# A bidirectional RWKV-7 layer on one Trainium2 core: copies ordered by PSUM bank, gate and residual rows fetched at the head of a round, and a fixed place for the loads of a stage

## The chip, the cores and the metric

The kernel runs on one core of one Trainium2 chip. The metric is the device time of one execution in microseconds (us), as the median of several runs. The engines are TensorE (PE, matmuls; PEld is its weight load), VectorE (DVE), ScalarE (ACT), GpSimd (POOL) and SyncE (SP), which here only issues DMAs. DMAs are also issued from the queues of ACT and POOL. An engine works through its own instructions in the order in which they stand; between engines there are only waits for data or for a buffer that has to come free.

## What is computed

One layer: an input projection, token shifts, a short convolution with gates, a two-way RWKV-7 scan over 128 context and 2048 latent tokens (8 heads of 64), and an output projection with a residual and a norm. The part that matters here is the scan:

```python
def step(S, inp):
    r_t, w_t, k_t, v_t, kk_t, a_t = inp
    s_kk = jnp.einsum('bdhij,bdhj->bdhi', S, kk_t)
    S = (S * w_t[..., None, :] - s_kk[..., :, None] * (kk_t * a_t)[..., None, :]
         + v_t[..., :, None] * k_t[..., None, :])
    return S, jnp.einsum('bdhij,bdhj->bdhi', S, r_t)
...
y = ys[:, 0] + jnp.flip(ys[:, 1], axis=1)
mean = jnp.mean(y, axis=-1, keepdims=True)
var = jnp.mean(jnp.square(y - mean), axis=-1, keepdims=True)
y = ((y - mean) * lax.rsqrt(var + GN_EPS)).reshape(b, t, A_WIDTH)
y = y * lp['gn_w'].astype(f32) + lp['gn_b'].astype(f32)
...
ya = ya.astype(x.dtype) * jax.nn.silu(g_a)
```

The kernel forms the scan by chunks of 64 tokens. Within a chunk the recurrence is a triangular system; its inverse is made once, and the state S then goes from chunk to chunk by matmuls.

## The kernel before

The program has three stages in time. The first makes the projections and spills the scan's operands to DRAM. The second is the scan. The third is the output projection; part of its matmuls (tile `psa`) is strewn into the scan to fill TensorE.

The scan is 17 stages (index s), each of 8 chunks in each of the two directions for one pair of heads (one of the 17 holds the context). A stage's parts are generators:

- `partL` (line 892) issues the loads of a stage's operands: `o` (two transfers of 512 KB, from `scr_ops`, line 907) and `a` (two of 128 KB, from `scr_lo`, line 914). They go into one of three sets of buffers, by s modulo 3.
- `partI` (917) loads the triangles (`ab`, four transfers, line 950) and solves them on GpSimd (`solve_steps`, 957; lines 960 to 980), which writes the inverse `scr_zt`. The buffer alternates between two, so the load for solve k waits until GpSimd is done with solve k-2. `partI(s + 7)` stands at the end of round s.
- `partW` (1036) makes two products: psF, masked by DVE into F (1066), and psG. A psG lies in two PSUM banks, one for each direction (`psG_0`, `psG_1`). DVE multiplies one half of each bank by a mask (1073, two instructions a bank), ACT copies the other half (1076, recorded at 846, two instructions a bank).
- `partU` (1079) transposes the inverse, multiplies it with `a` into psU; ACT copies psU into `zr` (1091, two instructions), and psW is the next product, from `zr`. psW is copied by ACT into `zb` (1101, recorded at 844).
- `partB` (1108) makes psX and four psE a half, masked by DVE (1136) and copied by ACT into `E`.
- `partS` (1140) is the chain over the chunks: psS from `sv` and `E`, then DVE scales psS into the next chunk's `sv` (1173).
- `finish` (1198) works up the output of one block: it fetches the gate rows `sg` (1215) and, three steps later, the residual rows `q` (1233, into a tile with the tag `w`), squares on ACT (1224), normalises on DVE (1227 to 1231), transposes on TensorE (psT), multiplies by the gate (1244, into a tile `yo`), adds q (1246) and stores to `scr_mixT` (1250).

A round s of the scan plays a list of letters (`ORDER`, 758): L is a step of partW(s+1), u and U of partU(s+1), b and B of partB of s and s+1, S of partS(s), `f`, `T` and `Y` steps of `finish`, a the projection's matmuls. Matmuls are kept in the order in which they were written (`pin`, `mm`), and some DMAs and ACT instructions are held behind the last matmul written (`now`). Such a tie is for the scheduler alone, which lays out each engine's order from a model of time; on the chip it is no wait. What isn't tied goes where the scheduler's model sees room.

In this text the rounds are numbered by s. In the trace, the psU of round 5 starts at 1140.3 us, of round 8 at 1216.1, of round 9 at 1240.6, of round 10 at 1270.8 and of round 11 at 1295.8.

Of the kernel before, what the change touches and what calls it, by code (L numbers as in the profile page):

```python
# [748 lines left out]

ROUND = "L b L u U S f b S b U S c b S c b L B L T S c B S B Y S c B S B".split()  # L750
ROUND_W = "L b L u U S f b S c b U S c b S c b c L B L T S B c S B Y c S B c S c B".split()
ROUND_M = "m L b L u U S f b S c b U S c b S b L B L T S B c S B Y c S m B S B".split()
ROUND_FILL = "L b a a L u U S f b S b U S b S b m L B a a L T S B S B Y S B S B".split()
ROUND_MORE = "m L b a a L u U S a a f b S b U S b S b L B a a L T S a a B S m Y B S B S B".split()
ROUND_ATT = "w m L b a a L u U S a a f b S b U w S b S b L B a a L T S a a B S m Y B S B S B".split()
ROUND_END = "w m L b a a L u U S a a f b S b U w S b b S L B a a L a a T w S B Y m S B S B w S B B".split()
ROUND_LAST = "f a a S w b S a x b S w a b T Y x S a b x".split()
ORDER = [ROUND, ROUND_W, ROUND_M] + [ROUND_FILL] * 10 + [ROUND_MORE, ROUND_ATT, ROUND_END, ROUND_LAST]
# [3 lines left out]
def phase2(K):  # L762
# [129 lines left out]
    def partL(s, after=None):  # L892
        st = Ctx()
        st.g = []
        st.low = B.low[s % LA]
        for gi, (d, units, blk) in enumerate(stages[s]):
            g = Ctx()
            st.g.append(g)
            g.d, g.units, g.blk = d, units, blk
            g.ops = B.ops[s % LA][d]  # L900
            src = S[f"ops{d}"][0:4:3]
            if blk is None:
                for k in range(2):
                    D(g.ops[:, k].rearrange("p (g u) t -> p g (u t)", u=2), src[k, :, 0:128].rearrange("(g p) t -> p g t", p=128))
            else:
                p, c0 = units[0]
                D(g.ops[:].rearrange("p k u t -> p k (u t)"), src[:, p * 128:(p + 1) * 128, c0 * 64:(c0 + 8) * 64].rearrange("k p t -> p k t"))
        for gi, g in enumerate(st.g):
            src = S["lo"][g.d]
            if g.blk is None:  # L910
                D(st.low[:, gi].rearrange("r (p u) i -> r p (u i)", u=2), src[:, 0:2].rearrange("(p r) u i -> r p (u i)", r=128))
            else:
                p, c0 = g.units[0]
                behind(D(st.low[:, gi], src[p * 128:p * 128 + 128, c0:c0 + 8]), after)
        return st
# [120 lines left out]
    def partW(s, st):  # L1036
# [7 lines left out]
        for n in range(2):  # L1044
# [22 lines left out]
            yield  # L1067
            ps = product(1, 0, "G")
            for gi, g in enumerate(st.g):
                us = half(g, n)  # L1070
                for h in range(2):
                    r = place(g.d, h)
                    V.tensor_tensor(g.gs[H[1 - h], g.op, h, us], ps[gi][r, :, 64:128], B.mG[r, g.d].unsqueeze(1).broadcast_to((64, 4, 64)), ALU.mult)  # L1073
                for h in range(2):
                    r = place(g.d, h)
                    copy(g.gs[H[1 - h], 0, h, us], ps[gi][r, :, 0:64])
            yield

    def partU(s, st):
# [10 lines left out]
        for r0, r1 in rows:  # L1090
            copy(zr[r1], pu[r1])
        yield
# [105 lines left out]
    def finish(p, blk, y):  # L1198
# [84 lines left out]
    def main():  # L1283
# [9 lines left out]
        for _ in range(3):  # L1293
            next(bb)
        sts[LA] = partL(LA, K.first)
        partI(7, O.solved)
        tail = iter(())
        side = dict(a=K.fill(), c=K.conv_weights(), m=K.mixes(), w=K.att_weights(), x=K.first_mixes())
        for s in range(NST):
# [8 lines left out]
            def play(tokens):  # L1308
                for c in tokens:
                    if c == "f":  # L1310
                        for f in todo:
                            for _ in range(3):
                                next(f, None)
                    elif c in "TY":
                        for f in todo:
                            next(f, None)
                    else:
                        next(gens[c])
                        if c == "S":
                            next(tail, None)  # L1320
# [3 lines left out]
            else:  # L1324
# [320 lines left out]
```

## Time and profile before

| | |
|---|---|
| runs | 1591.10, 1594.23, 1593.82 us (median 1593.82) |
| the profiled execution | 1593.89 us, its span 1592.1 us |
| TensorE busy | 1509.6 us (95%) |
| VectorE, ScalarE, GpSimd busy | 1120.7, 772.5, 586.8 us |
| granted TensorE clock | 0.984 of full speed, mean |
| DMA | 336.67 MB, 211 GB/s over the span |

The page and the views name an instruction by its line in the kernel, its engine and its tiles (out<-in). "x4" is a count; a time in brackets is how long the engine stood idle before it, and the arrow names what ended that. The SPq rows of the timeline are DMAs being issued, not the transfers themselves. `scr_...` are the scratch tensors in DRAM.

### The profile page before, as it was taken

What the parts mean: (1) busy time and instruction counts of PE and PEld (TensorE: products, weight loads), DVE (VectorE), ACT (ScalarE), POOL (GpSimd) and SP (SyncE); (2) the same over time, 40 slices, a digit from 0 to 9 for tenths busy, and PEclk for the clock granted to TensorE, in tenths of its full rate; (3) what the DMA queues carried; (4) which work ended last, traced back from release to release, by engine and by line L of the source; (5) the groups of instructions that cost most, each with busy time, mean ns of one, the idle gap of its engine ahead of it and who ended that gap; (6) DMA issues with size and microseconds to landing.
All of it is one profiled execution on the core that took longest, in us unless ns stands there. A gap on an engine that the chain in (4) does not pass through costs nothing.

```text
span 1592.1 us, 42472 instructions
## 1 busy us (share of the span) xinstructions
PE 1509.6 (95%) x17160; PEld 1382.9 (87%) x17160; DVE 1120.7 (70%) x2246; ACT 772.5 (49%) x1645; POOL 586.8 (37%) x1030
## 2 busy tenths in 40 slices
PE   6899999999999999999999989989999999999997
PEld 3799988999999999999989889977888788877886
DVE  5875978785646866757878788557677576677773
ACT  4553655462515453525535401566766666663331
POOL 0011212120202121202286567388888883012431
PEclk9899999999999999999999999999999999999999
DMA  9686758766555656464684976777676676558751
GB/s 376 199 297 219 266 188 303 254 224 234 166 171 171 205 177 217 164 214 171 208 256 158 282 233 208 211 205 213 182 209 191 192 203 188 138 160 314 247 177 66
DMA packets 242355, 336.67 MB, mean 211 GB/s; under 512 B 91688, under 2 KB 192296, under 8 KB 228080
## 3 DMA queue, kind: packets, MB, share of 16 engines
q1 hardware_dynamic: 233616, 323.27, 63.7%
q10 hardware_dynamic: 7344, 6.76, 1.4%
q0 software_dynamic: 1200, 3.93, 0.7%
q8 instruction: 135, 2.21, 0.6%
q14 instruction: 60, 0.49, 0.1%
HBM read 212.64 MB, written 121.26 MB: 210 GB/s over the span
## 4 chain that ended last, share of the span: by engine, by line
PE 44%; POOL 10%; DVE 8%; DMA 4%; ACT 3%; issue 3%; SPq 0%; DVEq 0%; ACTq 0%; POOLq 0%
PE psu L1446 7%; POOL zt L975 5%; POOL ztmp L972 3%; PE psE L855 3%; PE psS L855 2%; PE psa L1446 2%; PE mmg L166 1%; PE mmg L167 1%; PE mmg L168 1%; PE mmc L166 1%; PE mmc L167 1%; PE mmv L166 1%; PE mmv L167 1%; PE mmc L168 1%; PE mmv L168 1%
## 5 line engine op out<-in xcount | busy, mean ns | idle before, releaser
L975 POOL TENSOR_TENSOR zt<-zt,ztmp 128x30 f32<-128x30 f32 (+7 forms) x390 | 156.9, 402 | 30.6
L855 PE MATMUL psE<-fg 128*64 128x128 f32 x2176 | 147.6, 278 | 2.0 <-issue 2.0
L855 PEld LDWEIGHTS psE<-fg 128*64 128x64 f32 x2176 | 120.9, 140 | 6.0 <-issue 4.0
L855 PE MATMUL psS<-sv,E 128*64 128x64 f32 x2176 | 95.5, 229 | 21.7 <-DVE sv L1173 16.2
L329 POOL TENSOR_TENSOR shk<-rawl 128x384 f32<-128x384 f32 (+1 forms) x24 | 25.2, 1049 | 243.1 <-ACT rawl L325 223.2
L855 PEld LDWEIGHTS psS<-sv,E 128*64 128x64 f32 x2176 | 81.2, 140 | 35.0 <-DVE sv L1173 23.5
L846 ACT COPY E<-psE 128x256 f32<-128x256 f32 x136 | 50.0, 372 | 103.2 <-DVE E L1136 90.6
L1073 DVE TENSOR_TENSOR fg<-psG,consts 64x256 f32<-64x256 f32 x136 | 57.4, 422 | 55.7 <-PE psG L855 53.7
L972 POOL TENSOR_TENSOR ztmp<-ab,zt 128x60 f32<-128x60 f32 (+4 forms) x165 | 87.0, 527 | 12.9
L844 ACT ACTIVATE fg<-psX 64x512 f32<-64x512 f32 x136 | 80.5, 592 | 20.3 <-PE psX L855 17.8
L1446 PE MATMUL psu<-woh,mha 128*128 128x512 f32 x272 | 88.9, 396 | 0.0
L1570 POOL TENSOR_TENSOR z<-z,x 128x512 f32<-128x512 f32 x32 | 47.4, 1482 | 93.7 <-DVE z L1566 45.4
L329 POOL TENSOR_TENSOR shv<-rawl 128x384 f32<-128x384 f32 (+1 forms) x24 | 21.2, 882 | 162.5 <-ACT rawl L325 162.3
L1136 DVE TENSOR_TENSOR E<-psE,consts 128x256 f32<-128x256 f32 x136 | 56.6, 417 | 30.3 <-PE psE L855 28.6
L1173 DVE TENSOR_TENSOR sv<-psS,pc 64x128 f32<-64x128 f32 x262 | 65.8, 276 | 16.0 <-PE psS L855 14.1
L446 POOL COPY pcs<-pp 128x6 f32<-128x6 f32 (+1 forms) x48 | 25.0, 523 | 137.3 <-ACT pp L435 133.4
L846 ACT COPY fg<-psG 64x256 f32<-64x256 f32 x136 | 49.8, 366 | 49.0 <-DMA fg<-scr_ops 17.6
L166 PE MATMUL mmc<-h,w 128*128 128x384 f32 (+1 forms) x192 | 65.3, 340 | 5.9 <-ACT q1r L327 4.1
L166 PE MATMUL mmg<-h,w 128*128 128x384 f32 (+1 forms) x192 | 64.2, 334 | 3.8 <-ACT q1v L327 3.8
L167 PE MATMUL mmc<-h,w 128*128 128x384 f32 (+1 forms) x192 | 64.6, 336 | 0.0
L166 PE MATMUL mmb<-h,w 128*128 128x384 f32 (+1 forms) x192 | 62.9, 328 | 1.5 <-ACT ta L439 1.5
L166 PE MATMUL mmgb<-h,w 128*128 128x384 f32 (+1 forms) x192 | 64.0, 333 | 0.3 <-ACT q1r L327 0.3
(316 smaller groups left out, 5083.3 us busy)
## 6 DMA issues: line engine op xcount, KB each, us to landing
w<-scr_wsp SPq DMA_DIRECT2D x68, 1024.0 KB, 6.0
scr_wsp<-w SPq DMA_DIRECT2D x34, 1024.0 KB, 5.7
scr_ops<-pair SPq DMA_DIRECT2D x80, 384.0 KB, 3.9
wr<-in_win SPq DMA_DIRECT2D x34, 512.0 KB, 6.0
o<-scr_ops SPq DMA_DIRECT2D x32, 512.0 KB, 5.3
fg<-scr_ops SPq DMA_DIRECT2D x120, 128.0 KB, 3.8
x<-in_x SPq DMA_DIRECT2D x17, 512.0 KB, 3.5
wadas<-in_wada SPq DMA_DIRECT2D x8, 1024.0 KB, 9.9
```

What stands on the lines that cost most here:

```text
L166: T.matmul(ps[:, :n], w[:, 0, k], hh[:, 0, k, :n], start=k == 0, stop=False)
L167: T.matmul(ps[:, :n], w[:, 0, k], hh[:, 1, k, :n], start=False, stop=False)
L168: K.dense = T.matmul(ps[:, :n], w[:, 1, k], hh[:, 0, k, :n], start=False, stop=k == 7).ins
L844: P.activation(dst, src, AF.Copy, scale=-1.0)
L846: P.copy(dst, src)
L855: r = T.matmul(*a, start=True, stop=True, **k)
L972: eng.tensor_tensor(tv, ab[:, j:j + 2, j + 2:32].unsqueeze(1).broadcast_to((128, kn, 2, n)), zt[:, :kn, j:j + 2].unsqueeze(3).broadcast_to ...
L975: last = eng.tensor_tensor(zt[:, :kn, j + 2:32], zt[:, :kn, j + 2:32], tv[:, :, r], ALU.subtract).ins
L1073: V.tensor_tensor(g.gs[H[1 - h], g.op, h, us], ps[gi][r, :, 64:128], B.mG[r, g.d].unsqueeze(1).broadcast_to((64, 4, 64)), ALU.mult)
L1136: V.tensor_tensor(to(H[1]), of(H[1]), B.mE[:, g.d].unsqueeze(1).broadcast_to((128, 4, 64)), ALU.mult)
L1173: r = V.tensor_tensor(dst, sp[gi][0:64, q], B.pc[0:64, d, 2 * p:2 * p + 2, c:c + 1].broadcast_to((64, 2, 64)), ALU.mult)
L1446: r = T.matmul(ps[:], l[:, c], r, start=start and n == x == 0, stop=stop and n == 3 and x == 2)
```

## The change

Four edits.

1. **psG and psU on ACT.** The copies of a psG bank are tied behind that bank's masks, the next bank's masks behind the first's, and U's copies of psU behind the last of G's copies.
2. **finish.** `sg` and `q` are fetched together in a step of their own, which a new letter `g` at the head of a round plays. `q` gets a tile of its own (tag `yo`), and the product that went into `yo` goes back into the tile of `sg`, from which it is stored.
3. **The loads of a stage.** The call `partL(s + 4)` at the end of round s becomes `partL(s + 3)` at a new letter `P` in the middle of round s; the early call for stage 3 goes.
4. **Ties.** The loads of `o` and `a` are held behind the last matmul written, as other DMAs were.

```diff
-ROUND_FILL = "L b a a L u U S f b S b U S b S b m L B a a L T S B S B Y S B S B".split()
+ROUND_FILL = "g L b a a L u U S f b S b U S b S b m L B a a L T P S B S B Y S B S B".split()
...
-                D(g.ops[:].rearrange("p k u t -> p k (u t)"), src[:, p * 128:(p + 1) * 128, c0 * 64:(c0 + 8) * 64].rearrange("k p t -> p k t"))
+                now(D(g.ops[:].rearrange("p k u t -> p k (u t)"), src[:, p * 128:(p + 1) * 128, c0 * 64:(c0 + 8) * 64].rearrange("k p t -> p k t")))
...
-                behind(D(st.low[:, gi], src[p * 128:p * 128 + 128, c0:c0 + 8]), after)
+                r = D(st.low[:, gi], src[p * 128:p * 128 + 128, c0:c0 + 8])
+                behind(r, after)
+                now(r)
...
+            st.masked = None
             for gi, g in enumerate(st.g):
                 us = half(g, n)
                 for h in range(2):
                     r = place(g.d, h)
-                    V.tensor_tensor(g.gs[H[1 - h], g.op, h, us], ps[gi][r, :, 64:128], B.mG[r, g.d].unsqueeze(1).broadcast_to((64, 4, 64)), ALU.mult)
+                    m = V.tensor_tensor(g.gs[H[1 - h], g.op, h, us], ps[gi][r, :, 64:128], B.mG[r, g.d].unsqueeze(1).broadcast_to((64, 4, 64)), ALU.mult)
+                    behind(m, st.masked)
+                    st.masked = m.ins
                 for h in range(2):
                     r = place(g.d, h)
-                    copy(g.gs[H[1 - h], 0, h, us], ps[gi][r, :, 0:64])
+                    st.copied = P.copy(g.gs[H[1 - h], 0, h, us], ps[gi][r, :, 0:64])
+                    behind(st.copied, st.masked)
...
-            copy(zr[r1], pu[r1])
+            behind(P.copy(zr[r1], pu[r1]), st.copied.ins if O.line else None)
...
-        sg = place("sg")
+        sg, q = place("sg"), place("yo")
...
         fetch("sg", sg)
+        fetch("q", q)
+        yield
...
-        q = place("w")
-        fetch("q", q)
...
-        o = place("yo")
+        o = sg
...
-        sts[LA] = partL(LA, K.first)
...
+                    if c == "P":
+                        if s + LA < NST:
+                            sts[s + LA] = partL(s + LA)
+                    elif c == "g":
+                        for f in todo:
+                            next(f)
...
-            if s + LA + 1 < NST:
-                sts[s + LA + 1] = partL(s + LA + 1)
```

TensorE's and GpSimd's instructions stand in the same order as before, and DVE's too but for a few neighbours in the last rounds. What moves is on ACT and on SP.

ACT, around the psU of round 8 (`fg` is where psG's copies go, `zr` where U's go, `w` and `yss` belong to finish), before:

```order
L1224 ACTIVATE w_15278<-y_13845 128x512
L846 COPY fg_9817<-psG_0_0_15201 64x256 x2
L846 COPY zr_15227<-psU_15229 32x512 x2
L846 COPY fg_9818<-psG_1_0_15202 64x256 x2
L1228 ACTIVATE yss_15280<-yss_15280,geps 128x8
```

and of the change:

```order
L1232 ACTIVATE w_15271<-y_13839 128x512
L1081 COPY fg_9817<-psG_0_0_15196 64x256 x2
L1081 COPY fg_9818<-psG_1_0_15197 64x256 x2
L1097 COPY zr_15222<-psU_15224 32x512 x2
L1236 ACTIVATE yss_15273<-yss_15273,geps 128x8
```

The two copies of psG's second bank now stand ahead of U's two copies; so it is in 15 of the scan's rounds.

SP, from the end of round 8 into round 9 (`ab` are the triangles for a solve on GpSimd, `sg` and `w<-scr_q` the gate and residual rows for finish, `a` and `o` a stage's operands), before:

```order
L907 DMA o_9813<-scr_ops_58 128x2x512
L1250 DMA scr_mixT<-yo_15495 128x512
L1023 DMA fg_9817<-scr_ops_57 64x2x256
L1012 DMA sv_15658<-scr_vt 64x1024
L950 DMA ab_1099_15593<-scr_at 32x1x1024 x4
L1012 DMA sv_15660<-scr_vt 64x1024
L1023 DMA fg_9817<-scr_ops_57 64x2x256
L1023 DMA fg_9818<-scr_ops_58 64x2x256 x2
L914 DMA a_10979<-scr_lo 128x256
L1213 DMA sg_15791<-scr_sg 128x512
L914 DMA a_10979<-scr_lo 128x256
L1213 DMA w_15800<-scr_q 128x512
```

and of the change:

```order
L907 DMA o_9816<-scr_ops_58 128x2x512
L914 DMA a_10980<-scr_lo 128x256 x2
L1256 DMA scr_mixT<-sg_15130 128x512
L1025 DMA fg_9817<-scr_ops_57 64x2x256
L1219 DMA sg_15644<-scr_sg 128x512
L952 DMA ab_1093_15583<-scr_at 32x1x1024 x4
L1219 DMA yo_15645<-scr_q 128x512
L1014 DMA sv_15652<-scr_vt 64x1024
L1014 DMA sv_15654<-scr_vt 64x1024
L1025 DMA fg_9817<-scr_ops_57 64x2x256
L1025 DMA fg_9818<-scr_ops_58 64x2x256 x2
```

`sg` now stands ahead of `ab` and `q` right behind it; both were at the end of this piece. `a` has gone up to `o`. In two of the rounds (4 and 8) `sg` stands behind `ab` too.

SP, at the start of the scan (`a` and `o` of stages 1 to 4, `ab` of solve 6), before:

```order
L907 DMA o_10977<-scr_ops_57 128x2x512
L907 DMA o_10978<-scr_ops_58 128x2x512
L587 DMA scr_mixT<-ob_5_10789 128x320
L914 DMA a_10979<-scr_lo 128x256 x2
L914 DMA a_10980<-scr_lo 128x256 x2
L950 DMA ab_11007<-scr_at 32x1024 x4
L914 DMA a_9814<-scr_lo 128x256 x2
```

and of the change:

```order
L907 DMA o_10977<-scr_ops_57 128x2x512
L907 DMA o_10978<-scr_ops_58 128x2x512
L587 DMA scr_mixT<-ob_5_10789 128x320
L914 DMA a_10979<-scr_lo 128x256 x2
L907 DMA o_9815<-scr_ops_57 128x2x512
L907 DMA o_9816<-scr_ops_58 128x2x512
L914 DMA a_10980<-scr_lo 128x256 x2
L952 DMA ab_11007<-scr_at 32x1024 x4
```

The two `o` of stage 2 come here between the `a` of stages 1 and 2; before, they and those of stage 3 were issued some 15 to 50 us earlier, beside the end of the projections. The two of stage 3 now come later in round 0.

More of the change, by code (lines that the diff above doesn't have):

```diff
@@ L747 @@
 LA = 3
-ROUND = "L b L u U S f b S b U S c b S c b L B L T S c B S B Y S c B S B".split()
-ROUND_W = "L b L u U S f b S c b U S c b S c b c L B L T S B c S B Y c S B c S c B".split()
-ROUND_M = "m L b L u U S f b S c b U S c b S b L B L T S B c S B Y c S m B S B".split()
-ROUND_FILL = "L b a a L u U S f b S b U S b S b m L B a a L T S B S B Y S B S B".split()
[L754 to L757, printed above, removed]
+ROUND = "g L b L u U S f b S b U S c b S c b L B L T P S c B S B Y S c B S B".split()
+ROUND_W = "g L b L u U S f b S c b U S c b S c b c L B L T P S B c S B Y c S B c S c B".split()
+ROUND_M = "g m L b L u U S f b S c b U S c b S b L B L T P S B c S B Y c S m B S B".split()
+ROUND_FILL = "g L b a a L u U S f b S b U S b S b m L B a a L T P S B S B Y S B S B".split()
+ROUND_MORE = "g m L b a a L u U S a a f b S b U S b S b L B a a L T P S a a B S m Y B S B S B".split()
+ROUND_ATT = "g w m L b a a L u U S a a f b S b U w S b S b L B a a L T S a a B S m Y B S B S B".split()
+ROUND_END = "g w m L b a a L u U S a a f b S b U w S b b S L B a a L a a T w S B Y m S B S B w S B B".split()
+ROUND_LAST = "g f a a S w b S a x b S w a b T Y x S a b x".split()
 ORDER = [ROUND, ROUND_W, ROUND_M] + [ROUND_FILL] * 10 + [ROUND_MORE, ROUND_ATT, ROUND_END, ROUND_LAST]
@@ L903, in partL @@
                 for k in range(2):
-                    D(g.ops[:, k].rearrange("p (g u) t -> p g (u t)", u=2), src[k, :, 0:128].rearrange("(g p) t -> p g t", p=128))
+                    now(D(g.ops[:, k].rearrange("p (g u) t -> p g (u t)", u=2), src[k, :, 0:128].rearrange("(g p) t -> p g t", p=128)))
             else:
                 p, c0 = units[0]
-                D(g.ops[:].rearrange("p k u t -> p k (u t)"), src[:, p * 128:(p + 1) * 128, c0 * 64:(c0 + 8) * 64].rearrange("k p t -> p k t"))
+                now(D(g.ops[:].rearrange("p k u t -> p k (u t)"), src[:, p * 128:(p + 1) * 128, c0 * 64:(c0 + 8) * 64].rearrange("k p t -> p k t")))
         for gi, g in enumerate(st.g):
@@ L1309, in play @@
                 for c in tokens:
-                    if c == "f":
+                    if c == "P":
[4 more added lines that the diff above has]
+                            next(f)
+                    elif c == "f":
                         for f in todo:
@@ L1340, in main @@
         for f in pend:
-            for _ in range(3):
+            for _ in range(4):
                 next(f)
```

## The prediction

> **What bounds the kernel now.** I read the page first, then the stretches of single rounds, then the timelines of the one round that stands out, engine by engine, and last the start of the scan.
>
> ```profile
> PE 1509.6 (95%) x17160; PEld 1382.9 (87%) x17160; DVE 1120.7 (70%) x2246; ACT 772.5 (49%) x1645; POOL 586.8 (37%) x1030
> ```
>
> TensorE is the bound, and its order doesn't change. So an edit of copies and DMAs pays only where TensorE stands still or runs at a lower clock. The stretches of rounds 8, 9 and 10, which hold the same work, show such a place:
>
> ```profile
> core 0: us, PE busy (x) PEld busy (x) DVE busy (x) ACT busy (x) POOL busy (x), PEclk, DMA share, GB/s
> 1216.12:1240.55 24.43, 23.61 (x596) 20.70 (x592) 16.58 (x43) 18.34 (x39) 21.18 (x45) 1.00 0.76 217
> 1240.55:1270.83 30.28, 26.31 (x596) 23.38 (x593) 16.34 (x42) 17.75 (x38) 25.98 (x60) 0.89 0.65 176
> 1270.83:1295.77 24.94, 23.95 (x596) 20.79 (x592) 19.91 (x47) 15.43 (x34) 21.72 (x46) 1.00 0.77 222
> ```
>
> Round 9 takes 30.28 us, its neighbours 24.43 and 24.94 (mean 24.69): 5.6 us too long, at a granted clock of 0.89. TensorE's timeline in it:
>
> ```profile
> 1254.41 1.04 PE L855 MATMUL psE<-fg 128*64 128x128 f32 x16
> 1259.34 1.12 PE L855 MATMUL psS<-sv,E 128*64 128x64 f32 x16 [3.88 <-DVE sv L1173]
> 1260.25 1.92 PE L855 MATMUL psE<-fg 128*64 128x128 f32 x16
> ...
> 1265.32 1.04 PE L855 MATMUL psE<-fg 128*64 128x128 f32 x16
> ```
>
> It stands for 3.88 us, and then the same psE takes 1.92 instead of 1.04 us until the clock is back some 5 us later. Behind the wait stand DVE, SP and GpSimd, in this order:
>
> ```profile
> 1258.35 0.75 DVE L1244 SCALAR_TENSOR_TENSOR yo<-psT,gwh,sg 128x512 f32<-128x512 f32 x1 [3.19 <-DMA sg<-scr_sg]
> 1259.01 0.47 DVE L1173 TENSOR_TENSOR sv<-psS,pc 64x128 f32<-64x128 f32 x2
> ...
> 1259.74 0.73 DVE L1246 TENSOR_TENSOR yo<-yo,w 128x512 f32<-128x512 f32 x1
> ```
> ```profile
> 1232.95 0.33 SPq L1250 DMA_DIRECT2D scr_mixT<-yo  x1
> ...
> 1235.29 0.57 SPq L1012 DMA_DIRECT2D sv<-scr_vt  x1
> 1242.94 3.03 SPq L950 DMA_DIRECT2D ab<-scr_at  x4
> ...
> 1251.47 0.33 SPq L1213 DMA_DIRECT2D sg<-scr_sg  x1
> ...
> 1254.92 0.32 SPq L1213 DMA_DIRECT2D w<-scr_q  x1
> ```
> ```profile
> 1242.61 0.31 POOL L972 TENSOR_TENSOR ztmp<-ab,zt 128x60 f32<-128x60 f32 x1
> ```
>
> DVE stood 3.19 us for the gate rows, with the scan's `sv` behind. SP was free at 1235.86 (1235.29 + 0.57), but the load of `ab` waited 7.1 us until GpSimd had read the old triangles for the last time (1242.61 + 0.31), so the gate rows went out at 1251.47. GpSimd falls behind all through the scan: its solves start 28.3 us apart (1158.8 and 1187.1 in the next row), a round takes some 24.7.
>
> ```profile
> L960 POOL MEMSET zt<- x2: 526/527/528, 1158.8 to 1187.1; 128x512 f32 x2
> ```
>
> **The change part by part.** *Gate rows ahead (edit 2).* In round 9 `sg` would go out where SP was free, 7 us before the load that blocks it, at the latest when the store before it has landed: 1232.95 and the 4.4 us of the row below, 1237.4. Its 3.9 us bring it in by 1241.3; it is wanted at 1255.2 (1258.35 - 3.19). This wait goes, and with it the halved clock: -5.6, the difference of the rounds, in which the usual short wait behind L1244 stays.
>
> ```profile
> sg<-scr_sg SPq DMA_DIRECT2D x17, 256.0 KB, 3.9
> w<-scr_q SPq DMA_DIRECT2D x17, 256.0 KB, 5.3
> scr_mixT<-yo SPq DMA_DIRECT2D x17, 256.0 KB, 4.4
> ```
>
> The Trainium skill ("TensorE: Matmul & The Clock Gate", Part 1) has TensorE's clock halved after an idle window of about 3.4 us and restored after one of work. By that rule, as an estimate, the slow stretch would lose half of 3.4, so 1.7 us, and the gain would be 3.88 + 1.7 = 5.6 less the usual short wait; the round's own difference needs no rule.
>
> What is late next is q, which stands right behind `ab`. In round 9 it would go out at 1245.97 (1242.94 + 3.03) and land at 1251.3; L1246 would want it at 1259.74 - 3.19 = 1256.5. Room: 5.2. For round 10:
>
> ```profile
> 1270.49 1.73 SPq L950 DMA_DIRECT2D ab<-scr_at  x4
> ```
> ```profile
> 1287.47 0.67 DVE L1246 TENSOR_TENSOR yo<-yo,w 128x512 f32<-128x512 f32 x1
> ```
>
> q out at 1272.2, in at 1277.5, wanted at 1287.47 - 5.6 = 1281.9. Room: 4.4. So it is covered unless GpSimd gets later by more than that (below). I put 0.4 for it, with 0 and 3 as its ends.
>
> *The gate tile is also the output's (edit 2).* `sg` now waits for the last store to land, and SP with it, some 2 us of each round from 4 on. Behind it stand `ab`, q, `sv`, `fg`. `ab` is wanted only when GpSimd ends its present solve, `fg` a round later. Cover enough: 0.
>
> *ACT's order (edit 1).* The rows around the psU of round 8:
>
> ```profile
> 1216.12 1.20 PE L855 MATMUL psU<-zr,a 32*32 32x32 f32 x64
> 1216.23 1.75 DVE L1073 TENSOR_TENSOR fg<-psG,consts 64x256 f32<-64x256 f32 x4 [2.20 <-PE psG L855]
> 1217.17 0.74 ACT L846 COPY fg<-psG 64x256 f32<-64x256 f32 x2 [0.61 <-DVE fg L1073]
> 1217.94 1.18 ACT L846 COPY zr<-psU 32x512 f32<-32x512 f32 x2
> 1219.15 0.74 ACT L846 COPY fg<-psG 64x256 f32<-64x256 f32 x2
> ...
> 1220.39 0.79 PE L855 MATMUL psW<-zc,zr 32*32 32x32 f32 x38
> ```
>
> The second bank's copies can start when its masks end, 1217.98, take 0.74, and U's 1.18 then end at 1219.93 instead of 1219.12. psW starts at 1220.39: 0.46 us of cover are left. Nobody waits for the second bank, so nothing is gained either. Round 2 has less cover:
>
> ```profile
> 1064.69 0.74 ACT L846 COPY fg<-psG 64x256 f32<-64x256 f32 x2
> 1065.46 1.18 ACT L846 COPY zr<-psU 32x512 f32<-32x512 f32 x2
> 1067.23 1.20 PE L855 MATMUL psW<-zc,zr 32*32 32x32 f32 x64
> ```
>
> There U's copies end at 1067.4, 0.2 behind psW's start. I take +0.2 in all; the upper end is the whole shift of 0.81 in 15 rounds less 0.46 of cover, 5.3.
>
> The Trainium skill ("PSUM — Partial Sum Buffer", "PSUM bank collisions raise a hardware error") has any two engines' accesses to one bank and quadrant kept apart, reads included. The trace agrees: ACT's copy stood 0.61 us for DVE's masks of its bank. By that rule U's copies, which waited for TensorE alone, now queue behind DVE's last masks as well, which speaks against this edit; by the rows it is the 0.46 of cover above.
>
> *Stage operands (edits 3 and 4).* In the running rounds `o` stands where it stood and `a` half a round from its use: 0. The start of the scan is another matter. The four `o` of stages 2 and 3 (2 MB) were issued before it:
>
> ```profile
> 991.97 1.82 SPq L907 DMA_DIRECT2D o<-scr_ops  x3
> ...
> 1013.71 1.72 SPq L950 DMA_DIRECT2D ab<-scr_at  x4
> ```
> ```profile
> 1018.98 0.20 POOL L964 COPY dgp<-ab 128x16 f32<-128x16 f32 x1 [25.02 <-DMA ab<-scr_at]
> ```
> ```profile
> 1010.00:1015.00 5.00, 3.91 (x112) 3.33 (x106) 2.15 (x6) 1.93 (x6) 0.00 (x0) 1.00 0.74 210
> ...
> 1035.00:1040.00 5.00, 4.62 (x148) 4.19 (x138) 2.22 (x7) 4.83 (x11) 4.29 (x10) 1.00 1.07 329
> ...
> 1045.00:1050.00 5.00, 5.00 (x63) 4.78 (x60) 2.15 (x6) 1.88 (x4) 4.65 (x9) 0.50 0.85 221
> ```
>
> Now 1 MB stands ahead of `ab` for solve 6, for which GpSimd stood 25 us. At 210 GB/s that is up to 5 us by which every solve could be later; at a DMA share of 0.74 part of it fits in, and I take 2.5. Room for q in round 10 shrinks from 4.4 to about 2, with 0 at the far end.
>
> From 1005 to 1045 the transfers grow by about 0.8 MB (1 MB of `o` more, two `a` of 128 KB fewer). DMA was full there already, and round 1 paid for it:
>
> ```profile
> 1044.80 1.01 PE L855 MATMUL psS<-sv,E 128*64 128x64 f32 x14 [2.93 <-issue]
> ```
>
> TensorE stood for 2.93 us with nothing to wait for that the profile shows, and 5 us at 0.50 of its clock followed. 0.8 MB cost between 0 and 3.8 us (at 210 GB/s); `a` and `o` now also go out ahead of `ab` in that round, which may ease it. I take +1.0, nearer to the rows in which DMA has room; the lower end is below nothing, -5.4, if the stall goes (2.93 and half of 5.00).
>
> **The sum.** -5.6 + 0.4 + 0.2 + 1.0 = -4.0. The profiled execution took 1593.89 us (1592.1 of span, 1.8 around it), next to the median of 1593.82, so 1593.8 - 4.0 = 1589.8. About 0.2%, 3.2 us, is what a measurement of this kernel can tell from no change: faster means under 1590.6, slower over 1597.0.
>
> **The rivals.**
> - *The wait moves to q.* GpSimd starts up to 5 us later, q lies behind `ab`, and rounds 9 and 10 each stand up to 1.5 us in L1246. Too short to halve the clock by the rows (a stand of 3.88 did, the usual ones don't). For it: 28.3 against 24.7 us a round, and a faster round 9 makes the lag worse. Against it: 4 to 5 us of room. 3 us instead of 0.4: 1593.8 - 5.6 + 3 + 0.2 + 1.0 = 1592.4.
> - *Slower: the start of the scan.* One mechanism: 0.8 MB more in queues that were full. It decides once the transfers of round 0 arrive more than about 3 us late, so that TensorE's clock halves: 3.8 us of standing, 2.5 of half clock, and 3.8 more in round 1's stall, 10.1 in all. Against it: shares of 0.74 in part of that stretch. With the -5.6: 1593.8 + 4.5 = 1598.3.
> - *It does not do what it says.* `sg` goes ahead in the list, but waits there for the store's landing, or the stall of round 9 turns up in another round, since GpSimd's lag is untouched: 1593.8. Against it: the room of 14 us worked out above.
> - *The start is eased.* Round 1's stall goes too: 1593.8 - 5.6 - 5.4 + 0.4 + 0.2 = 1583.4.
>
> **How the numbers follow.** The forecast has 0.47, q 0.22, the slower start 0.13, no effect 0.10, the eased start 0.08. The range takes in all but the slower start and the edges: 1583 to 1597. Faster: 0.40 of the forecast's, which its own spread of 1587 to 1592 leaves under 1590.6, 0.02 of q's and 0.08: 0.50. Slower: 0.13 and 0.01 of the rest: 0.14. Same: 0.36.
>
> **What would show it.** Right: round 9 near 24.7 us with a clock of 1.00, no wait of L1244 for a DMA, `sg` issued ahead of `ab`, psW waiting for `zr` nowhere but in rounds 1 and 2, GpSimd's solve 6 starting at 1020 to 1023. Wrong: a wait of L1246 for `scr_q` in rounds 9 and 10; psW waiting for `zr` round after round; a stand of over 3 us, or a clock of 0.5, between 1010 and 1050; another round of 30 us.

## The result: 0.56% slower

| | before | after |
|---|---|---|
| median of 10 runs each, us | 1593.26 | 1602.37 |
| lowest to highest, us | 1589.64 to 1597.3 | 1596.05 to 1606.21 |
| ratio, 95% interval | | 1.0056, 1.0040 to 1.0071 |
| the profiled execution, us (span) | 1593.89 (1592.1) | 1604.49 (1602.4) |

The prediction said 1589.8 us, with a range up to 1597: the sign is wrong, and so is the range.

The rounds by the windows view (from psU to psU) show where the two profiled executions part. Before, then after, rounds 8, 9, 10, 11 and, further on, 14:

```profile
1216.12:1240.55 24.43, 23.61 (x596) 20.70 (x592) 16.58 (x43) 18.34 (x39) 21.18 (x45) 1.00 0.76 217
1240.55:1270.83 30.28, 26.31 (x596) 23.38 (x593) 16.34 (x42) 17.75 (x38) 25.98 (x60) 0.89 0.65 176
1270.83:1295.77 24.94, 23.95 (x596) 20.79 (x592) 19.91 (x47) 15.43 (x34) 21.72 (x46) 1.00 0.77 222
1295.77:1320.35 24.58, 23.60 (x597) 20.57 (x593) 18.25 (x44) 15.98 (x35) 21.25 (x48) 1.00 0.77 202
...
1372.25:1399.18 26.93, 26.93 (x608) 22.97 (x605) 19.91 (x49) 16.50 (x36) 2.51 (x2) 1.00 0.67 168
```
```profile
1214.27:1240.40 26.13, 24.11 (x597) 20.88 (x593) 17.09 (x43) 18.39 (x39) 22.65 (x50) 1.00 0.72 188
1240.40:1274.97 34.57, 28.13 (x597) 24.95 (x593) 16.40 (x42) 17.75 (x38) 29.67 (x68) 0.85 0.61 163
1274.97:1300.17 25.20, 24.15 (x596) 20.77 (x593) 19.81 (x47) 15.56 (x34) 21.95 (x47) 1.00 0.81 207
1300.17:1326.58 26.41, 24.22 (x597) 20.94 (x593) 18.34 (x44) 16.12 (x35) 22.85 (x51) 1.00 0.74 213
...
1378.80:1409.38 30.58, 28.72 (x608) 24.50 (x604) 20.21 (x50) 16.90 (x36) 2.49 (x2) 0.94 0.68 184
```

Round 9 starts at the same time in both (1240.55 and 1240.40). It was to fall from 30.28 to 24.7 us and rose to 34.57 (+4.3); round 11 adds 1.8 (with a stand of 1.2 us for which the profile names nothing) and round 14 3.7, rounds 10 and 12 0.3 each. Together they make the 10.3 us between the spans. Round 8 took 1.7 us longer too, but the rounds ahead of it had begun 0.9 us earlier and run 0.9 us faster, so in this pair of executions nothing of the loss lies ahead of round 9.

**Round 9 after the change.** DVE's two steps of `finish` (timeline of the changed kernel; the gate product is now L1250, the addition of q L1252):

```profile
1258.06 0.75 DVE L1250 SCALAR_TENSOR_TENSOR sg<-psT,gwh,sg 128x512 f32<-128x512 f32 x1
...
1259.46 0.67 DVE L1252 TENSOR_TENSOR sg<-sg,yo 128x512 f32<-128x512 f32 x1
```

Neither has an idle time in brackets: the wait of 3.19 us for the gate rows is gone, as predicted, and q is not late. TensorE stands all the same, now for ACT's copies of psG, and runs at half its clock behind it:

```profile
1265.27 1.98 PE L855 MATMUL psE<-fg 128*64 128x128 f32 x16 [4.19 <-ACT fg L1081]
```

ACT's own rows say what it did meanwhile (ACTq is a DMA issued from ACT's queue):

```profile
1256.01 0.57 ACT L1469 COPY z<-psa 128x512 f32<-128x512 f32 x1
1264.05 0.33 ACTq L1470 DMA_DIRECT2D scr_z<-z  x1
1264.47 1.52 ACT L1081 COPY fg<-psG 64x256 f32<-64x256 f32 x4 [7.90 <-DMA zc<-scr_zt]
```

The copy of z was done at 1256.58, and the store of z behind it was issued at 1264.05. ACT stood at the store, for a load of `zc` that has nothing to do with z. The same rows of the kernel before, which the prediction had not looked at:

```profile
1253.13 0.57 ACT L1460 COPY z<-psa 128x512 f32<-128x512 f32 x1
1259.56 0.33 ACTq L1461 DMA_DIRECT2D scr_z<-z  x1
1259.98 1.51 ACT L846 COPY fg<-psG 64x256 f32<-64x256 f32 x4 [6.28 <-DVE E L1136]
```

There ACT stood 6.28 us too, beside DVE's wait for the gate rows. The name behind the arrow is wrong: it was the store, issued 5.86 us after its data were ready.

**Why a store waits for a stranger's load.** Besides waits for data and for buffers there is a third kind here. The program gives the DMAs of SP and ACT eight completion semaphores in turn, in the order in which they were laid out, and issues none before the last one on its semaphore has landed. So each waits for the DMA eight places ahead, its neighbour in what follows. (In the traces of both kernels SP and ACT use the same eight; 636 of their issues follow one whose landing is recorded, and none of these goes out ahead of it.) The order in round 9, with the neighbour of z's store left of the bar:

```
before:        q  | zc zc mxc fg fg fg fg   | z's store
after:         zc | zc mxc fg fg fg fg o    | z's store
edits 1 and 2: a  | zc zc mxc fg fg fg fg   | z's store
```

Two waits of SP that the trace shows exactly, the first for a semaphore, the second for a tile, from the DMA issues of this stretch (size, time from issue to landing) and SP's queue:

```profile
scr_mixT<-sg SPq DMA_DIRECT2D x2, 256.0 KB, 7.6
...
yo<-scr_q SPq DMA_DIRECT2D x1, 256.0 KB, 9.3
```
```profile
1236.56 0.39 SPq L1256 DMA_DIRECT2D scr_mixT<-sg  x1
1237.04 0.58 SPq L1025 DMA_DIRECT2D fg<-scr_ops  x1
1244.19 0.32 SPq L1219 DMA_DIRECT2D sg<-scr_sg  x1
1247.06 2.73 SPq L952 DMA_DIRECT2D ab<-scr_at  x4
1249.83 0.51 SPq L1219 DMA_DIRECT2D yo<-scr_q  x1
...
1256.83 2.14 SPq L1054 DMA_DIRECT2D zc<-scr_zt  x2
1259.13 4.20 SPq L1430 DMA_DIRECT2D mxc<-scr_mixT  x1
```

q went out at 1249.83 and took 9.3: `mxc`, eight places behind it and with no use for it, went out at 1259.13. The output's store went out at 1236.56 and took 7.6: `sg`, which now shares its tile, went out at 1244.19. Then `ab` went out at 1247.06 (before: 1242.94), when GpSimd had read the old triangles; then everything behind it in a burst. The first `zc` went out at 1256.83, and z's store at 1264.05; the landing of `zc` itself isn't recorded, but the arrow of ACT's row above names it, and the store has its semaphore.

### The profile page after: what moved, and what is told of

Read it like the earlier page. It is cut to its first block, busy times and chain, and to the rows that moved or that the text cites. A ratio compares the mean times of both kernels' runs of the same rounds, so it can differ in the third digit from the quotient of the medians.

```text
span 1602.4 us, 42424 instructions
## 1 busy us (share of the span) xinstructions
PE 1508.4 (94%) x17160; PEld 1378.7 (86%) x17160; DVE 1130.0 (71%) x2246; ACT 775.6 (48%) x1645; POOL 585.7 (37%) x1030
## 4 chain that ended last, share of the span: by engine, by line
PE 42%; POOL 11%; DVE 10%; DMA 3%; issue 3%; ACT 2%; SPq 0%; ACTq 0%; DVEq 0%; POOLq 0%
PE psu L1455 8%; POOL zt L977 5%; POOL ztmp L974 4%; PE psE L855 3%; PE psa L1455 2%; PE psS L855 2%; DVE fg L977 1%; PE mmg L168 1%; PE mmg L167 1%; PE mmg L166 1%; PE mmv L166 1%; PE mmv L167 1%; PE mmv L168 1%; DVE fg L974 1%; PE psX L855 1%
## 5 line engine op out<-in xcount | busy, mean ns | idle before, releaser
L977 POOL TENSOR_TENSOR zt<-zt,ztmp 128x30 f32<-128x30 f32 (+7 forms) x390 | 156.6, 402 | 30.5
L855 PEld LDWEIGHTS psE<-fg 128*64 128x64 f32 x2176 | 121.1, 140 | 11.7 <-ACT fg L1081 7.1
L446 POOL COPY pcs<-pp 128x6 f32<-128x6 f32 (+1 forms) x48 | 21.3, 444 | 139.4 <-ACT pp L435 139.2
L166 PE MATMUL mmc<-h,w 128*128 128x384 f32 (+1 forms) x192 | 63.9, 333 | 5.9 <-ACT q1r L327 4.1
L166 PE MATMUL mmv<-h,w 128*128 128x384 f32 (+1 forms) x192 | 63.9, 333 | 0.3 <-ACT q1r L327 0.3
```

Source lines behind the costliest of these rows:

```text
L166: T.matmul(ps[:, :n], w[:, 0, k], hh[:, 0, k, :n], start=k == 0, stop=False)
L855: r = T.matmul(*a, start=True, stop=True, **k)
L977: last = eng.tensor_tensor(zt[:, :kn, j + 2:32], zt[:, :kn, j + 2:32], tv[:, :, r], ALU.subtract).ins
```

## The theories

A: what starts the stand is SP standing at `ab`; from there the gate rows are late for DVE (before), and by the shared semaphores z's store is late on ACT (both). B: the loss comes from the start of the scan, where GpSimd falls back. C: from SP's wait for the landing of the output's store. Later ones (D to I) are named in the expectations. The kernel before was run again beside each group of kernels; its median lay between 1590.98 and 1592.87 us, so the ratios compare better than the medians. A round of one profile is one execution: where two profiles of the same kernel were taken, both are told.

| kernel | median us | ratio to before, 95% | round 9, us |
|---|---|---|---|
| changed, z's store on SP | 1597.87 | 1.0029 (1.0019 to 1.0040) | 25.04 |
| edits 1 and 2 | 1595.36 | 1.0015 (1.0004 to 1.0026) | 32.65, 25.03 |
| edits 3 and 4 | 1599.00 | 1.0035 (1.0022 to 1.0047) | 33.30 |
| before, z's store on SP | 1592.79 | 1.0006 (0.9994 to 1.0018) | 34.45 |
| before, late ab | 1588.76 | 0.9975 (0.9962 to 0.9987) | 24.97, 29.68 |
| changed, late ab | 1595.51 | 1.0026 (1.0008 to 1.0044) | 31.85 |
| changed, z on SP, weights later | 1597.39 | 1.0035 (1.0022 to 1.0048) | 24.84 |
| changed, ab first | 1598.22 | 1.0026 (1.0015 to 1.0037) | 25.36 |
| changed, late ab, own output tile | 1597.26 | 1.0027 (1.0012 to 1.0042) | 25.72 |
| edit 1 | 1593.48 | 0.9999 (0.9986 to 1.0011) | 30.39 |
| changed without edit 4 | 1596.40 | 1.0026 (1.0014 to 1.0038) | 33.83 |
| edit 4 | 1603.25 | 1.0078 (1.0058 to 1.0097) | 28.77 |
| before, late ab for three, z on SP | 1588.00 | 0.9969 (0.9957 to 0.9982) | 24.33 |
| changed, all remedies | 1593.74 | 1.0016 (1.0002 to 1.0030) | 25.69 |
| changed without edit 4, remedies | 1589.97 | 0.9997 (0.9983 to 1.0011) | 25.19 |

## The experiments

**1. z's store on SP (changed kernel).**

```diff
-                        P.dma_start(S["z0"][i, :, HALF[h]], z[:])
+                        D(S["z0"][i, :, HALF[h]], z[:])
```

> The changed kernel; only the store of z (18 times, 256 KB) is issued from SP's queue instead of ACT's. Theory A: the loss is ACT standing at this store. A DMA shares its completion semaphore with the DMA eight places ahead of it in the program and is issued only when that one has landed; in round 9 of the changed kernel this is the first load of zc, in round 8 one of fg, both late because SP was held at ab. ACT then stands 7.9 and 4.3 us with the copies of psG behind it, and TensorE 4.19 and 1.19 us. With the store on SP, round 8 should take about 24.6 us, round 9 about 25 at a clock of 1.00: 1602.4 - 9.6 - 1.5 = 1591. Theory B, the start of the scan (GpSimd 4 us later, so everything behind ab is late): the loads stay as late as they are, round 9 stays at 33 to 35 us: 1601 to 1603. Theory C, SP held by the landing of the output's store ahead of sg: as B.

Round 9 and round 14 of this kernel:

```profile
1239.94:1264.98 25.04, 24.00 (x596) 20.77 (x592) 16.00 (x42) 17.46 (x37) 21.64 (x49) 1.00 0.58 135
1368.50:1401.85 33.35, 29.59 (x609) 25.36 (x605) 20.19 (x50) 16.88 (x36) 2.48 (x2) 0.90 0.65 174
```

Round 9 came out as theory A said, 25.04 us at a full clock, though `ab` was still issued 4.2 us behind the round's start (2.4 in the kernel before, whose round took 30.28). So late loads alone, as B and C have them, do not hold TensorE in this round. Round 8 fell by 0.3 us only, round 14 lost 2.8 more, and the whole fell by 4.5 us instead of 11.

**2. The same edit on the kernel before.**

> The kernel before; only the store of z is issued from SP's queue instead of ACT's. Theory A says that ACT stood 6.28 us at this store in round 9 of the kernel before as well (its neighbour eight places ahead is q), beside DVE's wait for sg, so that either alone holds TensorE. With the store on SP the copies of psG are no longer late, but DVE still waits 3.19 us for sg: TensorE's stand of 3.88 stays, round 9 stays at 29 to 30.5 us, 1592 to 1593.5. If the store was the only cause, round 9 falls to 25: 1588. If neither, no change: 1593.3.

The time did not change, as expected, but round 9 was longer, 34.45 us instead of 29 to 30.5. DVE's gate product:

```profile
1255.07 0.75 DVE L1244 SCALAR_TENSOR_TENSOR yo<-psT,gwh,sg 128x512 f32<-128x512 f32 x1 [6.84 <-DMA sg<-scr_sg]
```

Rounds 0 to 8 had taken 222.0 instead of 225.5 us, while GpSimd kept its pace: TensorE came to round 9 earlier and stood longer there. With ACT free, the gate rows alone hold it. The stand eats what the rounds ahead of it gain.

**3. Edits 1 and 2 alone; edits 3 and 4 alone.**

> The kernel before with edits 1 and 2 alone (order on ACT; gate and residual rows at the head of a round); the loads of a stage as before. Theory A: z's store now has a load of a eight places ahead, issued some 5 us before it, so ACT stands little; sg goes out ahead of ab; round 9 about 25 us instead of 30.3: 1593.3 - 5.4 = 1588. Theory B (start of the scan): the start is as before, so also about 1588. Theory C (SP waits some 7 us for the output's store ahead of sg, with ab behind it, round after round): ab and the loads behind it are late as in the changed kernel, round 9 stays over 30: 1593 to 1600.

> The kernel before with edits 3 and 4 alone (place and ties of the loads of a stage). Theory A: one load of o now stands ahead of z's store in the program, so the DMA eight places ahead is the first load of zc in round 9 and q in round 8; sg is still fetched late. ACT's stand of round 9 grows by some 4 us as in the changed kernel, and DVE's wait for sg lies beside it: round 9 at 33 to 36 us, total 1598 to 1602. Theory B: the loss comes at the start, in rounds 0 to 4, of which each stands longer; round 9 stays near 30: 1596 to 1600. Theory C: nothing to do with these edits: 1593.

With edits 1 and 2, DVE had no wait for the gate rows, but TensorE stood 4.74 us in round 9 for ACT, and ACT at z's store:

```profile
1250.59 0.57 ACT L1467 COPY z<-psa 128x512 f32<-128x512 f32 x1
1259.35 0.36 ACTq L1468 DMA_DIRECT2D scr_z<-z  x1
1259.80 1.51 ACT L1079 COPY fg<-psG 64x256 f32<-64x256 f32 x4 [8.64 <-DMA a<-scr_lo]
```

A as a mechanism holds (the neighbour is `a`, as the order says); my number for it did not: `a` too stood behind `ab` and went out between 1251.5 and 1254.1, only when ACT was ready for the store. The numbers (1595.36 us, round 9 at 32.65) lie where theory C had them, but not for its reason: `sg` had gone out at 1236.77, and `ab` followed at 1241.80, as GpSimd's last read of the old triangles ended (1241.78). In every profile with `ab` at its old place that read ends just ahead of `ab`, by 0.02 to 0.03 us. Edits 3 and 4 gave 1599.0 with round 9 at 33.30, as A said.

A second profile of edits 1 and 2 (recorded as `edits_1_2_z_on_sp`, though z's store is on ACT's queue in it):

> A repeat of the kernel with edits 1 and 2 alone, as a look at the spread of round 9 from one profile to another: 32.65 us the first time, 30 to 34 expected.

```profile
1241.83:1266.86 25.03, 23.95 (x597) 20.79 (x593) 15.90 (x42) 17.73 (x38) 21.61 (x47) 1.00 0.76 195
```

25.03 us, out of the expected 30 to 34, in the same kernel. `ab` was issued 1.6 us ahead of the round's start here, 4.2 us behind it in the first profile. Over the eight profiles in which DVE or ACT holds TensorE in round 9 and `ab` stands at its old place, the round lasts 27.1 to 28.6 us plus the time from its start to the issue of `ab` (0.1 to 6.8 us). So it ends some 28 us after GpSimd lets `ab` go, however early TensorE arrived.

**4. The load of ab half a round later**, for solves 15 and 16 (the letter I stands in the middle of the round):

```diff
+                    if c == "I":
+                        if s + 6 in (15, 16):
+                            partI(s + 6)
...
-            if 1 <= s and s + 7 < NST:
+            if 1 <= s <= 7:
                 partI(s + 7)
```

> The kernel before; the load of ab for solves 15 and 16 stands in the middle of rounds 9 and 10 instead of at the end of rounds 8 and 9. Theory A: what starts the stand of round 9 is SP standing 7.1 us at this load, until GpSimd has read the buffer for the last time; everything in SP's queue behind it (sg, sv, fg, zc) and, by the shared completion semaphores, ACT's store of z is late from there. GpSimd wants these triangles only a solve (28 us) later, so moving the load costs it nothing. Round 9 falls from 30.3 to about 24.7 us: 1592.9 - 5.6 = 1587.3. Theory D, the late DMAs of round 9 are late by the DMA engines' load and not by SP's stand: round 9 stays at 29 to 31, 1592 to 1594.

> The changed kernel with the same move of the load of ab for solves 15 and 16. Theory A: round 9 falls from 34.6 to about 25 us, with z's store still on ACT's queue: 1602.4 - 9.6 = 1592.8; what remains over the kernel before with the same move are rounds 8, 11 and 14 (1.7, 1.8 and 3.6 us). Theory B, the later start of GpSimd's solves costs time by itself: round 9 stays over 30: 1598 or more.

Round 9 of the kernel before with this edit:

```profile
1236.40:1261.37 24.97, 23.79 (x596) 20.80 (x592) 15.86 (x42) 17.66 (x38) 21.58 (x48) 1.00 0.75 202
```

24.97 us and 0.25% faster: SP's stand at `ab` is the root in the kernel before. In the changed kernel the median fell by 6.9 us (by the ratios 4.8), not 9.6. Its profiled execution is no good witness (1604.2 us, 8.7 above the median): round 9 lost its time there in three stands without a releaser. A second profile of the kernel before with this edit (recorded as `before_late_ab_z_on_sp`, with z's store on ACT's queue):

> A second profile of the kernel before with the late load of ab, as a look at the spread: round 9 at 24 to 26 us again, 1585 to 1591.

It took 1585.0 us, but round 9 took 29.7: a stand without a releaser of 1.96 us, then half clock. The expectation for the round failed.

**5. Round 14.** TensorE stands there for nothing that the profile names:

```profile
1389.28 0.39 PE L855 MATMUL psS<-sv,E 128*64 128x64 f32 x7 [1.86 <-issue]
```

The trace has the packets of TensorE's instruction fetch (16 KB each): the one ahead of this row was served from 1386.5 to 1387.8, 7.7 us into the round; in the kernel before the one at this place came 5.4 us into it. DMA was full: a share of 0.97 in the round's first 10 us, 0.64 before:

```profile
1378.80:1388.80 10.00, 8.62 (x242) 7.67 (x239) 6.63 (x18) 7.73 (x17) 1.12 (x1) 1.00 0.97 242
```
```profile
1372.25:1382.25 10.00, 10.00 (x278) 8.97 (x278) 6.86 (x19) 7.75 (x17) 1.25 (x2) 1.00 0.64 150
```

SP's queue ahead of it, changed kernel:

```profile
1368.42 1.11 SPq L907 DMA_DIRECT2D o<-scr_ops  x2
1369.58 0.94 SPq L914 DMA_DIRECT2D a<-scr_lo  x2
1370.62 0.57 SPq L1256 DMA_DIRECT2D scr_mixT<-sg  x1
1372.82 0.58 SPq L1025 DMA_DIRECT2D fg<-scr_ops  x1
1377.61 0.32 SPq L1219 DMA_DIRECT2D sg<-scr_sg  x1
```

Stage 16's operands (edit 3) stand ahead of the output's store, which lands late; `sg` waits for it (edit 2), SP stands 4.2 us, and the burst of the round's head begins 1.2 us ahead of the round (1378.80); with the tile of its own, below, it begins 5.3 us ahead (1369.88, the round at 1375.22). Two runs try this: the weights out of the burst (`w` moved in the letters of round 14; z on SP), and the output in another tile, so that SP does not stand:

```diff
-        o = sg
+        o = w
```

> The changed kernel with z's store on SP, and in round 14 the load of 512 KB of output weights moved from the head of the round to behind its sixth step. Theory E: the stand of 3.76 us in round 14 of the changed kernel with z's store on SP (1.86 us in the changed kernel), for which the trace shows no releaser, is TensorE's own instructions fetched late: 16 KB that lie behind the burst of gate rows, residual rows, weights and mix at the head of the round, which edit 2 made one load longer. Without the weights in that burst the stand goes, round 14 falls from 33.4 to about 27: 1597.9 - 6.3 = 1591.6. If the fetch is late for another reason, round 14 stays at 30 to 34: 1597 to 1598.

> The changed kernel with the late load of ab; and the output is formed in the tile of the squares instead of the tile of the gate rows, so the next gate rows no longer wait for the landing of the output's store. Theory G: in round 13 the store stands behind 1.25 MB of stage operands (edit 3), lands late, and SP waits some 5 us at the next gate rows; the burst behind it (gate and residual rows, weights, mix) then meets the fetch of TensorE's instructions in round 14. Without the wait the burst goes out some 5 us earlier, round 14 falls from 32.4 to 27 or 28 us: 1595.5 - 4.5 = 1591. If SP's wait is not the reason, round 14 stays at 30 to 33 us: 1595.

Round 14 fell from 33.35 to 28.66 us with the weights later, and from 32.40 to 27.18 with a tile of its own:

```profile
1375.22:1402.40 27.18, 27.18 (x609) 23.11 (x605) 20.12 (x50) 16.87 (x36) 2.50 (x2) 1.00 0.69 181
```

For the weights this shows little: with `ab` first (below) and neither remedy, round 14 took 28.56 us, so it varies that much by itself. For the tile it is better founded: 27.18, and 27.19 with all remedies (below), against 28.56 to 33.35 in the four kernels with the whole change and neither remedy (without edit 4 it is 27.65 without the tile and 28.01 with it). Neither whole time fell (1597.4 and 1597.3, where 1591.6 and 1591 were expected): stands without a releaser came up in other rounds (1.2 us at 1304, 1.4 at 1173; 2.1 at 1303, 1.8 at 1410).

**6. The start of the scan.** The changed kernel's rows there: a wait of TensorE for weights, one for the first states, and GpSimd's first step of solve 6:

```profile
991.59 0.44 PE L166 MATMUL mmgb<-h,w 128*128 128x384 f32 x1 [1.52 <-DMA w<-scr_wsp]
```
```profile
1017.23 0.45 PE L855 MATMUL psS<-sv,E 128*64 128x64 f32 x8 [1.56 <-DMA sv<-scr_sti]
```
```profile
1021.65 0.21 POOL L966 COPY dgp<-ab 128x16 f32<-128x16 f32 x1 [34.59 <-DMA ab<-scr_at]
```

Solve 6 starts 7.6 us behind the psU of round 0, before 4.0. The order of SP's queue has the 1 MB of `o` for stage 2 directly ahead of this `ab`, put there by edit 4.

```diff
-        sts[2] = partL(2, K.first)
         partI(6, K.first)
+        sts[2] = partL(2, K.first)
```

> The changed kernel; at the start of the scan the load of ab for solve 6 is issued ahead of the loads of o and a for stage 2 instead of behind them. In the profiles so far with a stand in round 9, the round lasts 27.4 to 28.4 us plus the time from its start to the issue of ab (2.4 us in the kernel before, 6.7 in the changed one). Theory A: edit 4 put the 1 MB of o for stage 2 directly ahead of ab for solve 6, GpSimd starts 7.6 us behind the first round instead of 4.0, and the lag lasts to round 9. With ab first, GpSimd starts about 4 us behind the first round, round 9 takes 30 to 32 us instead of 34.6: 1602.4 - 3.6 = 1598.8. Theory F, GpSimd's start does not matter: round 9 stays at 33 to 35 us: 1602.

1598.2, near the expected number, but not by the expected way; solve 6 starts 4.4 us behind the round. Round 9 was at 25.36, not 30 to 32: TensorE had stood 8.9 us in rounds 0 to 8 without a releaser (5.2 in the changed kernel), and came to round 9 1.6 us behind the issue of `ab`. The same number from another round is luck.

**7. The edits apart.** Edit 1 alone; the changed kernel without the ties of edit 4; edit 4 alone.

> The kernel before with edit 1 alone (order of the copies of psG and psU on ACT). The trace of the changed kernel has zr ready 3.9 us behind the start of psU in typical rounds and psW starting at 4.3, so the copies are hidden: 0 to +1 us, 1592 to 1594, and round 9 as in the kernel before. If the order on ACT costs what the prediction had as its upper end (0.35 us in each of 15 rounds): 1597.6.

> The changed kernel without edit 4 (the loads of o and a not held behind the last matmul written), edits 1 to 3 as they are. Its order has a load of a eight places ahead of z's store, as with edits 1 and 2 alone, and no o between stage 1's and ab for solve 6. Theory H, the ties are what costs: GpSimd starts about 4 us behind the first round, the waits at 990 and 1016 us go, z's store waits little: as with edits 1 and 2 alone, 1594 to 1596. Theory I, the place of the loads (edit 3) costs: 1599 to 1602.

> The kernel before with edit 4 alone. Theory H: as with edits 3 and 4 together, GpSimd 6 to 8 us behind the first round, round 9 at 32 to 34 us, TensorE waiting at 990 and 1016 us for loads that stand behind the o of stage 2: 1597 to 1600. Theory I: 1592 to 1594.

Edit 1 is worth nothing (0.9999). Edit 4 alone costs 0.78%, more than all four together and more than theory H expected; why more is open. The changed kernel without it still costs 0.26%: Theory H holds for half of the loss, not for all. z's store did not wait little there: ACT stood 10.9 us at it, and in that round q was late for DVE, which the prediction had as a rival:

```profile
1251.31 0.73 DVE L1250 TENSOR_TENSOR sg<-sg,yo 128x512 f32<-128x512 f32 x1 [2.87 <-DMA yo<-scr_q]
```

Where edit 4 loses is the start. In the ten profiles of kernels without edit 4, psU of round 0 starts at 1009.9 to 1015.0 (mean 1012.7); in the nine with it at 1013.4 to 1017.9 (1015.4). Round 0 then takes 20.5 to 20.9 us in all ten, and 21.5 to 24.3 in all nine, so that round 1 starts 4.8 us later by the means (1033.2 and 1038.1), of which round 1 gives 1.2 back. TensorE waits for the weights at 990 to 996 us in eight of the nine (0.6 to 1.7 us), for the first states in five (1.2 to 1.6), and in none of the ten. TensorE's stands without a releaser between 1014 and 1460 us sum to 3.3 to 11.7 us without edit 4 (mean 7.5), 6.2 to 16.8 with it (10.9). In the kernel with edit 4 alone they are spread over the scan:

```profile
PE psE L855 <- issue: 8.1, 7, 1.8
PE psF L855 <- issue: 3.3, 2, 1.7
PE psW L855 <- issue: 2.4, 4, 1.1
PE psS L855 <- issue: 2.2, 2, 1.3
```

**8. Remedies together.** The late `ab` for solves 14 to 16, and z's store on SP: on the kernel before; on the changed kernel with `ab` first and the own tile added; and on the changed kernel without edit 4, with the own tile.

> The kernel before with ab of solves 14, 15 and 16 loaded in the middle of rounds 8 to 10, and z's store on SP: SP stands at ab in none of the last rounds, and ACT never waits for another's load. Rounds 8 and 9 at 24.4 to 25.5 us: 1586 to 1588.5, against 1588.8 with the late load for solves 15 and 16 alone. If the late load of solve 14 starves GpSimd, its solves from 14 on start late and a round from 11 on waits for zc: 1592 or more.

> The changed kernel with all remedies: ab of solve 6 ahead of stage 2's loads, ab of solves 14 to 16 in the middle of the round, z's store on SP, the output in the tile of the squares. If the terms found so far are the whole loss: 1588 to 1590, next to the kernel before with its remedies. If more is lost in edits 2 to 4 (the fetch of TensorE's instructions meeting other bursts): 1593 to 1596.

> The changed kernel without edit 4 (so edits 1 to 3), with ab of solves 14 to 16 in the middle of the round, z's store on SP and the output in the tile of the squares. Theory H, what is left in the changed kernel with all remedies (1593.7) are the ties: 1588 to 1589.5, as the kernel before with its remedies (1588.0), so edits 1 to 3 are worth nothing once SP no longer stands. If edits 2 and 3 cost by themselves: 1592 to 1594. If edits 1 to 3 gain once round 9 is free: 1585 or less.

The first is the fastest kernel of the study, 1588.0 us, 0.31% (0.18 to 0.43) under the kernel before. Its rounds 8 and 9:

```profile
1212.41:1237.54 25.13, 23.93 (x596) 20.89 (x592) 17.02 (x43) 18.33 (x39) 21.82 (x47) 1.00 0.76 206
1237.54:1261.87 24.33, 23.51 (x596) 20.60 (x592) 15.86 (x42) 17.72 (x38) 21.08 (x47) 1.00 0.72 199
```

It is level with the late `ab` for two solves alone (0.9975, the intervals overlap), so neither the third late load nor the move of z's store adds anything that can be measured. The changed kernel with all remedies stays 0.16% above before, where its expectation put it if more was lost; without edit 4 it is level with before (1589.97 us, just over what theory H had). So edit 4 seems to cost some 3 us beyond the terms found (the two intervals just overlap), and edits 1 to 3 do not pay even with round 9 free: against the kernel before with its remedies (0.9969, 0.9957 to 0.9982) they stand at 0.9997 (0.9983 to 1.0011) with theirs, some 4.5 us behind, though the two were run in different groups. Where edits 1 to 3 lose that was not settled, nor how the rest of edit 4 divides over the fetch of instructions and the start.

## Why the prediction was wrong

- **"This wait goes, and with it the halved clock: -5.6."** This is the step that failed. The wait went (L1250 stands for nothing); the stand did not, since ACT stood 6.28 us at z's store in the same round of the kernel before, for the same cause. The prediction ended the chain at the wait that the profile named last and did not ask whether a second one lay beside it. That either wait is enough was shown both ways: with the gate rows early and the store on ACT TensorE stood 4.74 us (edits 1 and 2), with the store off ACT and the gate rows late 7.54 (z's store on SP in the kernel before). With SP's stand itself taken away, the round does fall to 24.97, and the whole by 0.25%.
- **Running rounds, stage operands: 0.** "`o` stands where it stood" was true of its time and false of its place: one `o` now stands ahead of z's store, which moved the store's neighbour from q to the later `zc`. With z's store on SP, 4.5 us of the loss are gone.
- **The store's landing ahead of `sg`: "some 2 us", cover enough.** It took 6.5 us in round 9 (store 1236.56, landed 7.6 later) and 4.2 ahead of round 14, where by theory G the late burst met TensorE's instruction fetch: 3.7 us in round 14. A tile of its own brings the round to 27.18.
- **Start of the scan: +1.0.** Mis-sized: the wait for weights and the one for the first states (1.5 and 1.6 us) are new, and by the means of kernels with and without edit 4 the loss is 2.7 us at the start of round 0 and 4.8 at that of round 1. In the two executions compared above it is -0.9 and 0.9, since the kernel before started late in its one. GpSimd's lag was forecast (2.5 us, up to 5; solve 6 starts at 1021.65 instead of 1018.98), but priced only in q's room; in fact round 9's end follows GpSimd. With `ab` first: 4.2 us less.
- **q: +0.4, ACT's order: +0.2.** Right, at 0, in the changed kernel: L1252 never stood for q, and edit 1 alone gives 0.9999. Without edit 4 q was late by 2.87 us in round 9, so that rival was near.
- **The rivals.** Nearest was "it does not do what it says": the stall stays because GpSimd's lag is untouched. It was given 0.10 and priced at no change; it had the cause, and missed that the lag grows by edit 4 and that the stand grows with it. "The start of the scan" had the place of a part of the loss (2.7 to 4.8 of 9.1 us, by the means), at 1598.3; its halved clock shows in round 0 or just ahead of it in five of the nine kernels with edit 4, not in the changed kernel's profile. No rival had ACT.

## What to carry to other kernels

Before a stall is counted as a gain, look at every engine's idle time in the same stretch, and at what released the cause: two waits that start from one late event are worth one. Where DMAs share completion semaphores in turn, a DMA that is put in or moved changes whom later ones wait for, and one that is issued from a compute engine's queue makes that engine wait: look up each such neighbour in the new order. And a load that must wait for a slow engine's buffer belongs as late in the queue as its consumer allows.

## What was not expected of the hardware

TensorE's own instructions come by DMA, in packets of 16 KB, and they can come late: 3.3 to 16.8 us of stands without a releaser in the scan of an execution. The link is close: in the 19 profiled executions TensorE stood 118 times for over 0.5 us without a releaser between 1014 and 1460 us, and each of these stands ended 1.2 to 1.9 us after such a packet had been served (a moment picked at random lies there in 13% of cases). That a busy DMA makes the packets late is likely, but not proved: from 3 us ahead of the stand to its end the DMA share was 0.94 in the median, and under 0.75 in a quarter of them. The Trainium skill ("Runtime: NRT & Kernel Launch", "Instruction fetch mechanics") calls this cost mostly hidden; these traces disagree where the DMA share is near 1.

The clock drops after shorter stands than forecast. In the 19 profiled executions, between 1014 and 1460 us, the clock fell to 0.50 in or soon after all 10 stands of TensorE over 3.1 us, but also 25 of 43 between 1.6 and 3.1 us and 10 of 60 between 1.1 and 1.6. Each of the 46 stretches at 0.50 in this part of the traces lasted 3.41 us or two or three times that. In round 14 of the changed kernel a stand of 1.86 us did:

```profile
1388.00:1390.00 2.00, 0.72 (x17) 0.72 (x18) 0.79 (x2) 1.56 (x4) 2.00 (x2) 1.00 1.02 234
1390.00:1392.00 2.00, 2.00 (x43) 1.83 (x42) 1.17 (x3) 0.37 (x1) 0.17 (x1) 0.67 0.52 114
1392.00:1394.00 2.00, 2.00 (x40) 1.73 (x34) 1.29 (x2) 0.00 (x0) 0.00 (x0) 0.50 0.44 128
```

The Trainium skill ("TensorE: Matmul & The Clock Gate", Part 1) has it after an idle window of about 3.4 us; by these runs that is where it becomes certain, not where it begins.
